# The low part of a weight unit, formed by a negated copy and an accumulating transfer

## The chip, the cores and the metric

The kernel runs on one core of a Trainium2 chip. The metric is the device time of one execution in microseconds (us), the median of several runs. The core has five engines with a queue each, which run at the same time and wait for each other by semaphores: TensorE (PE; its weight loads are shown as PEld), VectorE (DVE), ScalarE (ACT), GpSimd (POOL) and SyncE (SP). Sixteen DMA engines move data between the HBM and the SBUF. A transfer is issued from an engine's queue and tells by a semaphore that it has landed.

## The reference

One layer of a hybrid decoder, in float32, for 512 prompt tokens and 8 x 8 sample tokens, 576 in all, with a width of 1024. Cut to what matters:

```python
xn = rms_norm(h, g_mix)
z = xn @ w_in                                   # 1024 x 6144
b, c, hc, v = z[..., :o1], z[..., o1:o2], z[..., o2:o3], z[..., o3:o4]
gate_a, gate_b = sigmoid(z[..., o4:o5]), sigmoid(z[..., o5:])
ya, cb = gated_short_conv(b, c, hc, conv_buf, w_conv)
ya = ya @ w_out_conv                            # 1024 x 1024
yb, pb = multiscale_pool(v, pool_buf, pos0, w_pool, pool_scale)
h = h + (gate_a * ya + gate_b * yb) @ w_o       # 1024 x 1024
h = h + square(relu(rms_norm(h, g_mlp) @ w_up)) @ w_down   # 1024 x 4096, 4096 x 1024
gp = sigmoid(rms_norm(h, g_ple) @ w_ple_gate)   # 1024 x 1024
h = h + gp * (p @ w_ple_proj)                   # 256 x 1024
return rms_norm(h, g_final), new_conv, new_pool
```

The outputs are the tokens after the final norm and the new states of the convolution and of the pooling.

## The kernel before

The tokens stand in the free dimension, two halves of 288 columns, and the channels on the 128 partitions. A product of one tile of 128 output channels (`product`, L104) sums over eight operand tiles of 128 channels each. Every float32 operand is used as two parts, a = hi + lo, in the type float32r: `mm` (L93) multiplies hi x hi, then weight-hi x operand-lo, then weight-lo x operand-hi, for both halves. That makes 6 matmuls per operand tile and 48 per product.

The weights come as a stream of 139 units in the order of their use (L134 to L149). A unit holds what one product needs, 128 x 1024 numbers (512 KB); a unit of `w_pool` has 128 x 512 and serves two products of two operand tiles each, so 24 matmuls, and a unit of `w_pp` serves four such products. `Stream.next` (L127) is called at each product. It loads units ahead (`load_unit`, from SyncE's queue into one of four `raw` tiles) and splits the unit that will be used two products later. `split_unit` (L86) calls `split` (L66): ScalarE casts the raw unit to `hi`, and VectorE subtracts `hi` from the raw unit into `lo`. There are three `hi` and three `lo` tiles, so that unit u+3 can be written only when the matmuls of unit u are done. Five units near the end (`resident`) are split in halves into tiles of another pool by `split_unit_acts` (L89).

The stages run in this order: the first norm with three products whose weights are loaded apart as `fraw` (PSUM tiles `psf`); 21 units of the gated convolution; 8 of its gate and 8 of its output; four groups of the pooling branch with two pool units, two gate units and one `w_pool` unit each; 8 of the output projection; the MLP with four blocks of 8 up and 8 down units; the embedding with 2 units of `w_pp` and 8 of `w_pg`. After a product, ScalarE and VectorE take it out of the PSUM, work on it and split the result by `split_act` for the next stage; GpSimd sums squares for the norms (`ss`) and copies pieces of the states. A scheduler in the framework orders each engine's instructions from the program, so the order of a queue isn't always that of the code; the instructions of one engine run in that order, and one that waits holds what is behind it.

Of the kernel before, what the change touches and what calls it, by code (L numbers as in the profile page):

```python
# [8 lines left out]
F32R = mybir.dt.float32r  # L9
AF = mybir.ActivationFunctionType  # L10
ALU = mybir.AluOpType

P = 128
# [26 lines left out]
def tile_hybrid_step(ctx: ExitStack, tc: tile.TileContext, x, pt, vecs, rc, ident, sconv, spool, w_first, w_in,  # L40
                     w_pool, w_oc, w_o, w_up, w_down, w_pg, w_pp,
                     y_out, ncp, npp, ncs, nps):
    nc = tc.nc
# [5 lines left out]
    wsp = ctx.enter_context(tc.tile_pool(name="wsp", bufs=3))  # L49
# [12 lines left out]
    def as32(ap):  # L62
        return ap.bitcast(F32)

# [1 line left out]
    def split(src, shape, pool, tag, scale=None, hi_from=None):  # L66
        hi = pool.tile(shape, F32R, tag=tag, name="hi")
        lo = pool.tile(shape, F32R, tag=tag if pool is acts else tag + "l", name="lo")
        if scale is None:
            nc.scalar.copy(hi, src)  # L70
            nc.vector.tensor_tensor(out=lo, in0=src, in1=as32(hi), op=ALU.subtract)  # L71
        else:
            nc.scalar.mul(hi, src, scale)  # L73
            nc.vector.scalar_tensor_tensor(  # L74
                out=lo, in0=src, scalar=scale, in1=as32(hi), op0=ALU.mult, op1=ALU.subtract)
        return hi, lo
# [4 lines left out]
    def load_unit(ap):  # L81
        raw = wraw.tile([P, ap.shape[1]], F32, tag="raw", name="raw")
        nc.sync.dma_start(raw, ap)
        return raw

    def split_unit(raw):  # L86
        return [split(raw, [P, raw.shape[1]], wsp, "w")]

    def split_unit_acts(raw):  # L89
        n = raw.shape[1] // 2  # L90
        return [split(raw[:, i * n:(i + 1) * n], [P, n], acts, "act") for i in range(2)]

    def mm(outs, w, c, m, act, start, stop):  # L93
        """outs: pieces of PSUM, each with the part of the operand's columns that it belongs to."""
        n = w[0][0].shape[-1]
        wh, wl = (t[:, c % n:c % n + m] for t in w[c // n])
        for i, (wt, at) in enumerate(((wh, act[0]), (wh, act[1]), (wl, act[0]))):
            for o, cols in outs:
                nc.tensor.matmul(o, wt, cols(at), start=start and i == 0, stop=stop and i == 2)  # L99

    def both(ps):
        return [(ps[:, h, :HT], lambda t, h=h: t[:, h, :]) for h in range(NH)]

    def product(unit, operands, base=0, m=P, step=P):  # L104
        """One tile of outputs on partitions: sum over the operand tiles."""
        ps = psum.tile([P, NH, 512], F32, tag="ps", name="ps")
        n = len(operands)
        for k, a in enumerate(operands):
            c = base + k * step
            mm(both(ps), unit, c, m, a, k == 0, k == n - 1)  # L110
        return ps

# [1 line left out]
    class Stream:  # L114
        def __init__(self, aps, ahead=2, resident=()):
            self.resident = resident
# [3 lines left out]
        def fill(self, loads, splits):  # L120
            while len(self.raws) < min(loads, len(self.aps)):
                self.raws.append(load_unit(self.aps[len(self.raws)]))
            while len(self.parts) < min(splits, len(self.aps)):
                i = len(self.parts)
                self.parts.append((split_unit_acts if i in self.resident else split_unit)(self.raws[i]))

        def next(self):  # L127
            self.fill(self.used + 1 + self.ahead + 1, self.used + 1 + self.ahead)
# [19 lines left out]
    order += [w_pg[j] for j in range(NJ)]  # L148
    stream = Stream(order, resident=range(len(order) - NJ, len(order) - 3))  # L149

# [1 line left out]
    vec = const.tile([P, NV, NJ], F32, tag="vec", name="vec")  # L152
    nc.scalar.dma_start(vec, vecs)

# [6 lines left out]
    for j in range(NJ):  # L161
# [4 lines left out]
        if j % 2 == 0:  # L166
            raw = wraw.tile([P, 2, 3 * P], F32, tag="raw", name="fraw")
# [16 lines left out]
    xg, first = [], []  # L184
    for j in range(NJ):
        if j == 0:
            hi, lo = (acts.tile([P, NH, HT], F32R, tag="act", name=n) for n in ("hi", "lo"))
# [17 lines left out]
    sp = const.tile([P, NJ, DB, PB], F32, tag="sp", name="sp")  # L205
    nc.sync.dma_start(sp, spool)

# [1 line left out]
    class Rms:  # L209
        def __init__(self, n=NH, width=HT, chunk=HT // 3):  # L210
            self.n, self.width, self.chunk, self.parts = n, width, chunk, []
# [14 lines left out]
                self.parts[0] = s  # L226

        def tokens(self):
            """Sums with tokens on partitions, and 1 / rms there."""
            n, m = len(self.at), self.chunk  # L230
            self.ps = ps = psum.tile([P, NH, 512], F32, tag="ps", name="psn")
            sums = ps[:m, 0, self.width:self.width + n]
            for i, (h, c) in enumerate(self.at):
                for k, a in enumerate(self.parts):
                    nc.tensor.matmul(  # L235
                        sums[:, i:i + 1], a[:, h, c:c + m], ones32[:, 0:1],
                        start=k == 0, stop=k == len(self.parts) - 1)
            rt, ms, y, t = (tmp.tile([m, n], F32, tag=g, name=g, bufs=2) for g in ("rt", "ms", "ry", "rz"))
            nc.scalar.activation(rt, sums, AF.Sqrt, bias=epst[:m], scale=1.0 / D)
            nc.vector.tensor_scalar(out=ms, in0=sums, scalar1=1.0 / D, scalar2=EPS, op0=ALU.mult, op1=ALU.add)  # L240
            nc.vector.reciprocal(y, rt)
            nc.vector.tensor_tensor(out=t, in0=y, in1=y, op=ALU.mult)
            nc.vector.scalar_tensor_tensor(out=t, in0=t, scalar=-0.5, in1=ms, op0=ALU.mult, op1=ALU.mult)
            nc.vector.scalar_tensor_tensor(out=y, in0=t, scalar=1.5, in1=y, op0=ALU.add, op1=ALU.mult)
            self.y = y

        def spread(self):
            """The same on all partitions, in PSUM."""
            m = self.chunk
            for i, (h, c) in enumerate(self.at):  # L250
                nc.tensor.matmul(  # L251
                    self.ps[:, h, c:c + m], self.y[:, i:i + 1].broadcast_to([m, P]), idt[:m, :m],
                    start=True, stop=True)
            return self.ps[:, :self.n, :self.width]
# [7 lines left out]
            nc.scalar.activation(out2, r, AF.Square)  # L262
            return out, out2

# [1 line left out]
    stat = Rms()  # L266
    for j in range(NJ):
        stat.add(xs[j])
# [1 line left out]
    for k in range(NJ):  # L270
        for u in range(3):
            mm(both(ps0[u]), [first[k]], u * P, P, xg[k], k == 0, k == NJ - 1)
        if k == 5:
            stat.tokens()
        if k == 6:
            r1, r1s = stat.copies(stat.spread(), "r", "rs")
# [1 line left out]
    ncp_t = const.tile([P, NJ, CW - 1], F32, tag="ncp", name="ncp_t")  # L278
    npp_t = const.tile([P, NJ, PB], F32, tag="npp", name="npp_t")

# [1 line left out]
    ya_in = []  # L282
    for j in range(NJ):
        ps_c = ps0[0] if j == 0 else product(stream.next(), xg)
        c = tmp.tile([P, NH, HT], F32, tag="t", name="c")
        nc.vector.tensor_tensor(out=c, in0=halves(ps_c), in1=r1s, op=ALU.mult)
        ps_h = ps0[1] if j == 0 else product(stream.next(), xg)
        u = tmp.tile([P, CEXT], F32, tag="ext", bufs=4, name="u")
        us = u[:, CE:].rearrange("p (b t) -> p b t", b=DB)
# [13 lines left out]
        for k in range(1, CW):  # L303
            nc.vector.scalar_tensor_tensor(
                out=cv[:, :n], in0=u[:, k:k + n], scalar=v(W_CONV + k, j), in1=cv[:, :n],
                op0=ALU.mult, op1=ALU.add)
        ps_b = ps0[2] if j == 0 else product(stream.next(), xg)
        bt = tmp.tile([P, NH, HT], F32, tag="t", name="bt")
        nc.vector.tensor_tensor(out=bt, in0=halves(ps_b), in1=r1, op=ALU.mult)
# [8 lines left out]
            op=ALU.mult)  # L318
        ya_in.append(split_act(ya))

# [1 line left out]
    mix = []  # L322
    for j in range(NJ):
        ps = product(stream.next(), xg)
        z = tmp.tile([P, NH, HT], F32, tag="t", name="z")
# [5 lines left out]
        ps = product(stream.next(), ya_in)  # L331
        nc.vector.tensor_tensor(out=mix[j], in0=halves(ps), in1=mix[j], op=ALU.mult)

# [1 line left out]
    merged = []  # L335
    for g, w in enumerate(WINDOWS):
        pooled = []
        for i in range(2):
# [14 lines left out]
            s, d = e, 1  # L353
            while d < w:
                q = tmp.tile([P, PEXT], F32, tag="ext", bufs=4, name="q")
                lo = 2 * d - 1
                nc.vector.tensor_tensor(
                    out=q[:, lo:], in0=s[:, lo:], in1=s[:, lo - d:PEXT - d], op=ALU.add)
                s, d = q, 2 * d
# [19 lines left out]
        for i in range(2):  # L379
            ps = product(stream.next(), xg)  # L380
            z = tmp.tile([P, NH, HT], F32, tag="t", name="zb")
# [14 lines left out]
    for o, t in ((ncp, ncp_t), (ncs, sc), (npp, npp_t), (nps, sp)):  # L396
        nc.sync.dma_start(o, t)

# [1 line left out]
    stat = Rms()  # L400
    hg = []
    for j in range(NJ):
# [2 lines left out]
        hg.append(split_act(xs[j], v(G_MLP, j)))  # L405
        stat.add(xs[j])

# [1 line left out]
    accs = [None] * NJ  # L409
    stat3 = Rms()  # L410
    hg2 = []
    for b in range(NFB):
        sq = []
        for j in range(NJ):
# [5 lines left out]
            a = tmp.tile([P, NH, HT], F32, tag="t", name="a")  # L420
# [20 lines left out]
                hg2.append(split_act(xs[j], v(G_PLE, j)))  # L441
                stat3.add(xs[j])

# [1 line left out]
    proj = []  # L445
    for i in range(2):
        w = stream.next()
# [23 lines left out]
    for h, (a, b) in enumerate(((0, cut), (cut, NT))):  # L471
        for j in range(NJ):
# [10 lines left out]
            z = tmp.tile([P, 1, b - a], F32, tag="t", name="z1")  # L483
# [98 lines left out]
```

## Time and profile before

| | before |
|---|---|
| median of 3 runs (range) | 927.73 us (927.15 to 928.21) |
| span of the profiled execution, first to last instruction | 926.5 us |
| its mean granted TensorE clock | 0.994 |
| DMA: bytes read from HBM, written | 77.01 MB, 2.99 MB |
| DMA: mean rate over the span | 87 GB/s |

The profile is of one execution on the chip; its own time beyond the span is not recorded, and the median of the runs lies 1.2 us above the span. In the profile's lines a group reads "line engine operation out<-in", with the shape and type, how many times it ran, its busy time and the mean of one, and the engine's idle time just ahead of it with what ended that. In a timeline a row begins with its start and its duration in us. In the slices a digit is the busy share of a fortieth of the span in tenths.

### The profile page before, as it was taken

How to read it: one execution, taken by the hardware profiler on the slowest of the kernel's cores; microseconds unless marked ns; L12 is line 12 of the kernel's file. 1: busy time of each engine (PE TensorE's matmuls, PEld its weight loads, DVE VectorE, ACT ScalarE, POOL GpSimd, SP SyncE). 2: the span in 40 equal slices, each digit the busy share in tenths (PEclk: the TensorE clock that was granted, in tenths of full speed). 3: DMA queues.
4: the chain of work that ended last, by engine and by line, in shares of the span. 5: the costliest groups of instructions: out<-in, count | busy, mean ns of one | idle time of the engine just before them, and what ended most of it. 6: DMA issues, size and time to landing. Idle time of an engine off the chain costs nothing.

```text
span 926.5 us, 15543 instructions
## 1 busy us (share of the span) xinstructions
PE 913.4 (99%) x6842; PEld 911.5 (98%) x6842; DVE 431.6 (47%) x570; ACT 289.8 (31%) x384; POOL 98.3 (11%) x118
## 2 busy tenths in 40 slices
PE   8999999999999999999999999999999999999995
PEld 7999999999999999999999999999999999999995
DVE  7645445333246687743342133332443334567555
ACT  6422212322113222333433233211331133335532
POOL 5110001000011221023000000000000000021253
PEclk9999999999999999999999999999999999999997
DMA  6422222322322222322222222222222222222102
GB/s 227 155 92 76 84 92 69 94 88 73 92 61 88 68 92 96 112 79 91 69 90 71 91 79 82 91 70 91 87 73 92 74 86 92 94 92 84 54 22 82
DMA packets 26290, 80.98 MB, mean 87 GB/s; under 512 B 3312, under 2 KB 7024, under 8 KB 26224
## 3 DMA queue, kind: packets, MB, share of 16 engines
q1 hardware_dynamic: 26080, 79.98, 26.4%
q8 instruction: 53, 0.87, 0.4%
q14 instruction: 13, 0.11, 0.0%
q10 hardware_dynamic: 144, 0.03, 0.0%
HBM read 77.01 MB, written 2.99 MB: 86 GB/s over the span
## 4 chain that ended last, share of the span: by engine, by line
PE 97%; DVE 1%; issue 1%; DMA 1%; SPq 0%; DVEq 0%; ACT 0%; ACTq 0%
PE ps L99 89%; PE psg L99 6%; PE psf L99 1%; PE psn L251 1%; DVE lo L71 1%; DMA xall<-x 1%; PE psn L235 1%; DVE xall L464 0%; SPq L169 0%; DVE lo L74 0%; SPq L163 0%; DVEq L564 0%; DVE gp L491 0%; DVE xall L493 0%; DVE sq L218 0%
## 5 line engine op out<-in xcount | busy, mean ns | idle before, releaser
L99 PE MATMUL ps<-lo,hi 128*128 128x288 f32 x2064 | 442.2, 296 | 0.0
L99 PE MATMUL ps<-hi 128*128 128x288 f32 x2064 | 442.1, 296 | 0.0
L99 PE MATMUL ps<-hi,lo 128*128 128x288 f32 x2064 | 441.8, 296 | 0.0
L99 PEld LDWEIGHTS ps<-hi,lo 128*128 128x128 f32 x2064 | 332.7, 189 | 0.0
L99 PEld LDWEIGHTS ps<-lo,hi 128*128 128x128 f32 x2064 | 332.7, 189 | 0.0
L99 PEld LDWEIGHTS ps<-hi 128*128 128x128 f32 x2064 | 332.6, 189 | 0.0
L70 ACT CAST hi<-raw 128x1024 fp32r<-128x1024 f32 (+1 forms) x144 | 144.8, 1008 | 468.3 <-PE ps L99 400.9
L71 DVE TENSOR_TENSOR lo<-raw,hi 128x1024 fp32r<-128x1024 f32 (+1 forms) x144 | 169.3, 1179 | 157.0 <-ACT hi L70 150.4
L437 DVE TENSOR_TENSOR acc<-ps,acc 128x576 f32<-128x576 f32 x24 | 18.2, 758 | 74.3 <-PE ps L99 74.3
L225 POOL TENSOR_TENSOR ss<-sq 128x576 f32<-128x576 f32 (+2 forms) x5 | 7.2, 1434 | 416.4 <-ACT sq L220 416.4
L225 POOL TENSOR_TENSOR ss<-ss,sq 128x576 f32<-128x576 f32 (+2 forms) x29 | 38.5, 1327 | 70.3 <-ACT sq L220 56.8
L99 PE MATMUL psg<-hi 128*128 128x320 f32 (+1 forms) x128 | 38.1, 298 | 0.0
L99 PE MATMUL psg<-lo,hi 128*128 128x320 f32 (+1 forms) x128 | 37.9, 296 | 0.0
L99 PE MATMUL psg<-hi,lo 128*128 128x320 f32 (+1 forms) x128 | 37.9, 296 | 0.0
L71 DVE TENSOR_TENSOR lo<-a,hi 128x576 fp32r<-128x576 f32 x32 | 24.3, 759 | 23.6 <-ACT hi L70 23.6
L70 ACT CAST hi<-a 128x576 fp32r<-128x576 f32 x32 | 21.6, 675 | 43.6 <-DVE a L423 43.6
L220 ACT ACTIVATE sq<-xall 128x576 f32<-128x576 f32 (+2 forms) x39 | 22.7, 585 | 19.5 <-DVE xall L493 19.5
L74 DVE SCALAR_TENSOR_TENSOR lo<-xall,vec,hi 128x576 fp32r<-128x576 f32 x23 | 21.7, 946 | 7.9 <-ACT hi L73 7.9
L99 PEld LDWEIGHTS psg<-hi 128*128 128x128 f32 x128 | 24.3, 190 | 0.0
L99 PEld LDWEIGHTS psg<-lo,hi 128*128 128x128 f32 x128 | 24.3, 190 | 0.0
L99 PEld LDWEIGHTS psg<-hi,lo 128*128 128x128 f32 x128 | 24.3, 190 | 0.0
L423 DVE TENSOR_TENSOR a<-a 128x576 f32<-128x576 f32 x32 | 24.1, 752 | 0.0
(98 smaller groups left out, 444.3 us busy)
## 6 DMA issues: line engine op xcount, KB each, us to landing
raw<-w_in SPq DMA_DIRECT2D x45, 512.0 KB, 3.4
raw<-w_up SPq DMA_DIRECT2D x32, 512.0 KB, 3.4
raw<-w_down SPq DMA_DIRECT2D x32, 512.0 KB, 3.5
raw<-w_oc SPq DMA_DIRECT2D x8, 512.0 KB, 3.4
raw<-w_o SPq DMA_DIRECT2D x8, 512.0 KB, 3.5
raw<-w_pg SPq DMA_DIRECT2D x8, 512.0 KB, 3.5
xall<-x SPq DMA_DIRECT2D x7, 288.0 KB, 5.2
fraw<-w_first SPq DMA_DIRECT2D x8, 192.0 KB, 5.1
```

What stands on the lines that cost most here:

```text
L70: nc.scalar.copy(hi, src)
L71: nc.vector.tensor_tensor(out=lo, in0=src, in1=as32(hi), op=ALU.subtract)
L74: nc.vector.scalar_tensor_tensor(out=lo, in0=src, scalar=scale, in1=as32(hi), op0=ALU.mult, op1=ALU.subtract)
L99: nc.tensor.matmul(o, wt, cols(at), start=start and i == 0, stop=stop and i == 2)
L220: nc.scalar.activation(sq, t, AF.Square)
L225: nc.gpsimd.tensor_tensor(out=s, in0=self.parts[0], in1=sq, op=ALU.add)
L235: nc.tensor.matmul(sums[:, i:i + 1], a[:, h, c:c + m], ones32[:, 0:1], start=k == 0, stop=k == len(self.parts) - 1)
L251: nc.tensor.matmul(self.ps[:, h, c:c + m], self.y[:, i:i + 1].broadcast_to([m, P]), idt[:m, :m], start=True, stop=True)
L423: nc.vector.tensor_tensor(out=a2, in0=a, in1=a, op=ALU.mult)
L437: nc.vector.tensor_tensor(out=accs[j], in0=halves(ps), in1=accs[j], op=ALU.add)
```

## The change

`split_unit` no longer calls `split`. ScalarE writes `hi` as before, and then writes the raw unit times -1 into `lo`, rounded to float32r as `hi` is, so that `lo` holds minus `hi`. A transfer issued from GpSimd's queue then reads the unit from the HBM a second time and adds it to what stands in `lo`. The subtraction on VectorE is gone for the 134 units that go this way; the five resident units, the first weights `fraw` and all activations are split as before. The comments that the diff takes out of other places have no effect and are left out here.

```diff
-    def split_unit(raw):
-        return [split(raw, [P, raw.shape[1]], wsp, "w")]
+    def split_unit(raw, ap):
+
+        shape = [P, raw.shape[1]]
+        hi = wsp.tile(shape, F32R, tag="w", name="hi")
+        lo = wsp.tile(shape, F32R, tag="wl", name="lo")
+        nc.scalar.copy(hi, raw)
+        nc.scalar.mul(lo, raw, -1.0)
+        nc.gpsimd.dma_start(lo, ap, accum_op=ALU.add)
+        return [(hi, lo)]
...
             while len(self.parts) < min(splits, len(self.aps)):
                 i = len(self.parts)
-                self.parts.append((split_unit_acts if i in self.resident else split_unit)(self.raws[i]))
+                if i in self.resident:
+                    self.parts.append(split_unit_acts(self.raws[i]))
+                else:
+                    self.parts.append(split_unit(self.raws[i], self.aps[i]))
```

The changed lines move the numbers of all lines behind them: in the changed kernel L91 is the cast to `hi` of a unit, L92 the negated copy into `lo`, L93 the transfer, and what stood at L225 or L384 is L235 or L394.

ScalarE at the start of the stream, before. `raw` is a weight unit, `rt` belongs to the first norm, and `r` and `rs` are its copies from the PSUM:

```order
L70 CAST hi<-raw 128x1024
L239 ACT_TABLE_LOAD
L239 ACTIVATE rt<-psn,epst 96x6
L70 CAST hi<-raw 128x1024
L258 COPY r<-psn 128x576
L262 ACTIVATE rs<-psn 128x576
L70 CAST hi<-raw 128x1024
```

The same place in the changed kernel:

```order
L91 CAST hi<-raw 128x1024
L249 ACT_TABLE_LOAD
L249 ACTIVATE rt<-psn,epst 96x6
L92 ACTIVATE lo<-raw 128x1024
L91 CAST hi<-raw 128x1024
L92 ACTIVATE lo<-raw 128x1024
L268 COPY r<-psn 128x576
L272 ACTIVATE rs<-psn 128x576
L91 CAST hi<-raw 128x1024
L92 ACTIVATE lo<-raw 128x1024
```

The first negated copy stands behind `rt`, and the second one ahead of `r`.

GpSimd at the same place, before: the sums of squares of the first norm, and pieces of the convolution's state (`u`, `sc`, `ncp_t`):

```order
L225 TENSOR_TENSOR ss<-ss,sq 128x576 x6
L291 COPY u<-sc 128x8x2
L298 COPY ncp_t<-u 128x2
L299 COPY sc<-u 128x16
L290 MEMSET u 128x2
```

In the changed kernel:

```order
L235 TENSOR_TENSOR ss<-ss,sq 128x576 x6
L301 COPY u<-sc 128x8x2
L93 DMA lo<-w_in 128x1024 x2
L308 COPY ncp_t<-u 128x2
L93 DMA lo<-w_in 128x1024
L309 COPY sc<-u 128x16
L300 MEMSET u 128x2
```

Two transfers are issued ahead of the copy that waits for the convolution's first tile, and the third one behind it.

ScalarE in the last group of the pooling branch, before. `pl` is an operand of the group's last product, `gb` a gate, `t` a merged result:

```order
L70 CAST hi<-raw 128x512
L70 CAST hi<-pl 128x576
L70 CAST hi<-raw 128x1024
L384 ACTIVATE gb<-zb 128x576
L70 CAST hi<-pl 128x576
L70 CAST hi<-raw 128x1024
L384 ACTIVATE gb<-zb 128x576
L70 CAST hi<-raw 128x1024
L70 CAST hi<-t 128x576 x2
```

In the changed kernel, from the cast of the same `w_pool` unit on:

```order
L91 CAST hi<-raw 128x512
L92 ACTIVATE lo<-raw 128x512
L91 CAST hi<-raw 128x1024
L70 CAST hi<-pl 128x576
L394 ACTIVATE gb<-zb 128x576
L92 ACTIVATE lo<-raw 128x1024
L91 CAST hi<-raw 128x1024
L92 ACTIVATE lo<-raw 128x1024
L394 ACTIVATE gb<-zb 128x576
L91 CAST hi<-raw 128x1024
L70 CAST hi<-t 128x576
L92 ACTIVATE lo<-raw 128x1024
```

The negated copy of the unit that is cast right after the `w_pool` unit stands behind the operand `pl` and the gate `gb`; the next one stands right behind its cast.

## The prediction

> **What bounds the kernel now.** I read the page's busy shares and slices first, then the chain that ended last, in order of time.
>
> ```profile
> span 926.5 us, 15543 instructions
> PE 913.4 (99%) x6842; PEld 911.5 (98%) x6842; DVE 431.6 (47%) x570; ACT 289.8 (31%) x384; POOL 98.3 (11%) x118
> PE   8999999999999999999999999999999999999995
> PEclk9999999999999999999999999999999999999997
> ```
>
> ```profile
> 29.06 2.02 PE psf L99 x15
> 31.08 409.60 PE ps L99 x3072
> ...
> 861.37 33.22 PE psg L99 x234
> ...
> 899.27 14.81 PE psg L99 x123
> 914.10 0.43 DVE z L484
> ```
>
> TensorE is busy in every slice but the first and the last, at full clock, and from 29 to 914 us the chain is matmuls alone: 3072 of them stand in one piece. VectorE, which the change relieves, has no step in the chain between 29 and 914 us. So nothing can be won in the middle, and the question is only whether TensorE comes to wait for a low part. The pace is 409.60 / 3072 = 0.1333 us a matmul, 6.40 us for a unit of 48, and 3.20 us for a unit of w_pool with 24. The first matmuls that read a low part are the fifth and sixth of a unit, 0.53 us after its start.
>
> **What is removed and added.** These are the two groups that split, from the page; a group with "+1 forms" mixes shapes.
>
> ```profile
> L70 ACT CAST hi<-raw 128x1024 fp32r<-128x1024 f32 (+1 forms) x144 | 144.8, 1008 | 468.3 <-PE ps L99 400.9
> L71 DVE TENSOR_TENSOR lo<-raw,hi 128x1024 fp32r<-128x1024 f32 (+1 forms) x144 | 169.3, 1179 | 157.0 <-ACT hi L70 150.4
> ```
>
> Of the 144, 10 are halves of the five resident units and stay; 134 go. VectorE loses about 134 x 1.2 = 160 us, all of it beside matmuls: worth nothing. ScalarE gets 134 negated copies. The trace has none; I take 1.05 us, the cast of the same shape below, since a relu and a cast of 576 columns there take 0.65 and 0.68. ScalarE goes from 290 to about 430 us of 926, still far from a bound. GpSimd's queue and the DMA engines get 134 accumulating transfers, which read the weights from HBM a second time.
>
> **The unknown: T, from issue to landing of one accumulating transfer.** The trace has no such transfer and none issued by GpSimd; every queue in it that carries data is a hardware one. The nearest rows:
>
> ```profile
> raw<-w_in SPq DMA_DIRECT2D x45, 512.0 KB, 3.4
> xall<-x SPq DMA_DIRECT2D x7, 288.0 KB, 5.2
> raw<-w_pool SPq DMA_DIRECT2D x4, 256.0 KB, 2.7
> q1 hardware_dynamic: 26080, 79.98, 26.4%
> ```
>
> 512 KB plain lands in 3.4 us, 256 KB in 2.7: so 2.0 fixed and 1.4 per 512 KB. The lowest value is 3.4, if reading the old contents and adding were free. With two reads of 512 KB side by side it is 2.0 + 2.8 = 4.8; with the two passes one behind the other 2 x 3.4 = 6.8. The slowest pace of a large load in the trace is 288 KB in 5.2 us; 1 MB at that pace takes 18 us, my upper end. Between these I take the middle of the two forms of a second pass, T = 5.8, nearest to the row of the same unit, and keep 3.4 and 18.
>
> [...]
>
> **Where T is hidden: the regular stages.** ScalarE in the MLP:
>
> ```profile
> 641.19 1.05 ACT L70 CAST hi<-raw 128x1024 fp32r<-128x1024 f32 x1 [5.35 <-PE ps L99]
> 647.59 1.05 ACT L70 CAST hi<-raw 128x1024 fp32r<-128x1024 f32 x1 [5.35 <-PE ps L99]
> 648.55 0.65 ACT L421 ACTIVATE a<-ps 128x576 f32<-128x576 f32 x1
> 650.60 0.68 ACT L70 CAST hi<-a 128x576 fp32r<-128x576 f32 x1 [1.41 <-DVE a L423]
> ```
>
> The high part of unit u+3 starts when unit u ends (three buffers), here at 647.59. Units u+1 and u+2 then run 2 x 6.40, and the low part is read at 647.59 + 12.80 + 0.53 = 660.9. In the changed order the relu stands between the cast and the negated copy: 647.59 + 1.05 + 0.65 + 1.05 = 650.3, when the transfer is issued. It is hidden as long as T is under 10.6. Behind it on GpSimd in this stage stand only the next units' transfers; in the stages with `ss` sums or state copies these wait at most for the issue, and their readers are a unit away.
>
> **Where it is tightest: the pool stage,** since a unit of w_pool is half as long. First ScalarE, then one row of TensorE:
>
> ```profile
> 373.30 1.05 ACT L70 CAST hi<-raw 128x1024 fp32r<-128x1024 f32 x1 [4.48 <-PE ps L99]
> 374.84 0.69 ACT L384 ACTIVATE gb<-zb 128x576 f32<-128x576 f32 x1 [0.49 <-DVE zb L382]
> 375.43 0.66 ACT L70 CAST hi<-pl 128x576 fp32r<-128x576 f32 x1
> 379.70 1.05 ACT L70 CAST hi<-raw 128x1024 fp32r<-128x1024 f32 x1 [3.60 <-issue]
> ...
> 389.30 1.05 ACT L70 CAST hi<-raw 128x1024 fp32r<-128x1024 f32 x1 [1.86 <-PE ps L99]
> ```
>
> ```profile
> 383.45 0.43 PE L99 MATMUL ps<-hi,lo 128*128 128x288 f32 x2
> ```
>
> The unit whose high part starts at 373.30 has its low part read at 383.45. In the new order two more ScalarE instructions come ahead of its negated copy: 373.30 + 1.05 + 0.66 + 0.69 + 1.05 = 376.8, so T up to 6.6 is hidden. The next one starts at 379.70 and its product at 389.30: 389.30 + 0.53 - (379.70 + 2.10) = 8.0. The three earlier groups have no pool operand between and stand at 8.0 too. With 5.8 this stage costs nothing; 0.8 us is what the first place has to spare.
>
> **Where it is not hidden: the first stream unit.** ScalarE, then VectorE, GpSimd and TensorE:
>
> ```profile
> 23.70 1.05 ACT L70 CAST hi<-raw 128x1024 fp32r<-128x1024 f32 x1 [3.07 <-DVE lo L71]
> 24.77 1.28 ACT L239 ACT_TABLE_LOAD   x1
> 26.06 0.26 ACT L239 ACTIVATE rt<-psn,epst 96x6 f32<-96x6 f32 x1
> 27.12 1.05 ACT L70 CAST hi<-raw 128x1024 fp32r<-128x1024 f32 x1 [0.80 <-PE psf L99]
> 29.09 0.64 ACT L258 COPY r<-psn 128x576 f32<-128x576 f32 x1 [0.93 <-PE psn L251]
> 29.63 0.66 ACT L262 ACTIVATE rs<-psn 128x576 f32<-128x576 f32 x1
> ```
>
> ```profile
> 24.78 1.23 DVE L71 TENSOR_TENSOR lo<-raw,hi 128x1024 fp32r<-128x1024 f32 x1 [0.62 <-ACT hi L70]
> 30.38 0.76 DVE L286 TENSOR_TENSOR c<-psf,rs 128x576 f32<-128x576 f32 x1 [0.95 <-ACT rs L262]
> ```
>
> ```profile
> 21.28 0.54 POOL L291 COPY u<-sc 128x16 f32<-128x16 f32 x1
> ```
>
> ```profile
> 30.92 0.43 PE L99 MATMUL ps<-hi 128*128 128x288 f32 x2
> 31.45 0.43 PE L99 MATMUL ps<-hi,lo 128*128 128x288 f32 x2
> ```
>
> Before, the low part of the first unit is done at 24.78 + 1.23 = 26.0, and TensorE reads it at 31.45. After, the negated copy stands behind `rt` and ends at 26.32 + 1.05 = 27.4; GpSimd is free since 21.8 and issues. What stays hidden is 31.45 - 27.4 = 4.0 us. With T = 5.8 the part lands at 33.2: **TensorE waits 1.8 us**. The second negated copy delays `r` and `rs`: the second cast moves from 27.12 to 27.4, then 28.5, copy to 29.5, `r` and `rs` together 1.2 to 30.7. TensorE starts the unit at 30.92, so this costs nothing, and `c` about 0.4 us later is not waited for before the next product. The second unit is read 6.40 later, at 37.9: its transfer, issued at 29.5, has 8.4. Once the stream has slipped by 1.8 us it is not caught up, since TensorE has no idle time to give back.
>
> The sum against the profiled execution: 926.5 + 1.8 = 928.3. The median of the runs shown, 927.73, lies 1.2 above its span, so **929.5**, 0.2% more. About 0.2% (1.9 us) is what a measurement of this kernel can tell from no change, and the forecast lies right on that bound.
>
> **The rivals.**
> - *No wait, hence not slower.* T is 4.0 or less, the adding being free as in the lowest end: the first unit lands before 31.45, time 927.7. For it speaks that a plain load has 3.4; against it the second read. It decides at T = 4.0, at 31.45 us.
> - *Later than the pool stage allows.* T between 6.6 and 10.6. At T = 9 the first unit costs 5.0, the last group 2.4, and the other three groups 1.0 each (the second unit of a group is carried by the slip of the first): 10.4 us, 938. At 10.6 it is 6.6 + 4.0 + 7.8 = 18.4, 946.
> - *The transfers become the bound.* T over 10.6, or more engine time than there is: loads take 26.4% of 926.5, some 1.75 us for each of 139 units, so an accumulating one has 6.40 - 1.75 = 4.6, 2.6 times a load. Past that, each us costs 134 / 3 = 45 us: 1010 at T = 12, and near 1280 at my upper end of 18. Against it: two reads make 2, not 2.6.
> - *A shared port.* Beside GpSimd's sum a VectorE subtraction took three times as long:
>
> ```profile
> 4.34 0.56 DVE L71 TENSOR_TENSOR lo<-fraw,hi 128x384 fp32r<-128x384 f32 x1
> 10.33 1.78 DVE L71 TENSOR_TENSOR lo<-fraw,hi 128x384 fp32r<-128x384 f32 x1
> ```
>
> ```profile
> 9.96 1.73 POOL L225 TENSOR_TENSOR ss<-ss,sq 128x576 f32<-128x576 f32 x1 [0.18 <-ACT sq L220]
> ```
>
> If issuing a transfer is held up likewise for one VectorE instruction, 1.2 us, T is 7.0 where VectorE is busy. At the first unit only short steps on 96 x 6 numbers are left on VectorE, so the price is 0.4 us at the last pool group: 929.9. [...]
> - *Faster.* Only if a lighter VectorE ended a wait on the chain; the chain has none between 29 and 914 us.
>
> **How the numbers follow.** Forecast (T 4.0 to 6.6, 927.7 to 930.3) 0.45; no wait 0.10; shared port 0.05; pool stage late 0.18; transfers the bound 0.19; faster 0.03. A second read is close to certain, hence the weight on the forecast, but a first transfer of a kind that the trace does not have can be far dearer than its bytes, hence the last cases. Of the forecast half lies on each side of T = 5.8: same is 0.10 + 0.22 = 0.32, slower 0.23 + 0.05 + 0.18 + 0.19 = 0.65, faster 0.03. The range of the likeliest case is 927.7 to 930.3; over all it reaches from 927.0 up to the end of the pool-stage case, 948, which leaves out 0.03 below and most of the 0.19 above.
>
> **What would show it.** Right: issue-to-landing of `lo<-w_in` near 5.8 us, one wait of TensorE near 31.5 us of T - 4.0, released by that transfer, and no other; ScalarE near 430 us; DMA share about 26% plus a half to the double of it. Wrong: waits of TensorE every third unit (T over 10.6), or in the pool stage (over 6.6), a GpSimd that is long busy with each issue, or no wait at all.

## The result, and the profile after

| | before | changed |
|---|---|---|
| median of four runs each (range), us | 927.73 (927.15 to 928.21) | 937.53 (933.01 to 939.09) |
| span of the profiled execution, us | 926.5 | 937.3 |
| mean granted TensorE clock | 0.994 | 0.991 |

The changed kernel is slower: the ratio is 1.0096, with a 95% interval of 1.0069 to 1.0123, so 9 us at the middle; the medians lie 9.8 us apart. The profiled execution of the changed kernel is the slowest of its four. The forecast was 929.5, in a range of 927.0 to 948.0.

The page of the changed kernel, its head and its slices:

```profile
span 937.3 us, 15857 instructions
PE 917.3 (98%) x6842; PEld 914.4 (98%) x6842; DVE 278.8 (30%) x436; ACT 408.6 (44%) x518; POOL 195.4 (21%) x252
PE   8799999999999999999999999999999999999995
PEclk9899999999999999999999999999999999999997
```

VectorE has lost 153 us of work and ScalarE has gained 119, and neither matters. What matters is one slice of TensorE that fell from 9 to 7, and one of its clock that fell from 9 to 8. The waits of TensorE for transfers follow, with total, times and the longest; then the transfers, with their number, size and median time from issue to landing:

```profile
PE ps L106 <- DMA lo<-w_in: 5.4, 2, 5.3
PE ps L106 <- DMA lo<-w_o: 1.6, 1, 1.6
```

```profile
q0 software_dynamic: 19296, 69.21, 42.2%
q1 hardware_dynamic: 26080, 79.98, 28.5%
raw<-w_in SPq DMA_DIRECT2D x45, 512.0 KB, 4.1
lo<-w_in POOLq DMA_DIRECT2D x45, 512.0 KB, 7.6
lo<-w_pg POOLq DMA_DIRECT2D x3, 512.0 KB, 5.6
lo<-w_pool POOLq DMA_DIRECT2D x4, 256.0 KB, 5.4
```

T, the time from issue to landing of an accumulating transfer, is 7.6 us here, and 5.6 for the last three, of `w_pg`. The three waits listed add up to 7.0 us, and none is listed for any other of the 134 transfers. The chain of work names transfers that ended late:

```profile
27.52 9.39 DMA lo<-w_in
...
361.73 8.11 DMA lo<-w_in
...
385.96 8.11 DMA lo<-w_o
```

How much of the loss lies where is read from the starts of the products' readers (minimum, median and maximum of their duration in ns, then the first and the last start in us). First two rows of before, then two of the changed kernel:

```profile
L286 DVE TENSOR_TENSOR c<-ps,rs x7: 751/757/757, 37.7 to 152.7; 128x576 f32<-128x576 f32 x7
L404 DVE TENSOR_TENSOR xall<-ps,xall x8: 758/758/758, 389.5 to 434.3; 128x576 f32<-128x576 f32 x8
```

```profile
L296 DVE TENSOR_TENSOR c<-ps,rs x7: 758/758/758, 45.7 to 160.9; 128x576 f32<-128x576 f32 x7
L414 DVE TENSOR_TENSOR xall<-ps,xall x8: 758/758/758, 400.3 to 445.1; 128x576 f32<-128x576 f32 x8
```

The first stream unit is finished 45.7 - 37.7 = 8.0 us later than before, the last of this stage 160.9 - 152.7 = 8.2 later, and the first unit of the output projection 400.3 - 389.5 = 10.8 later, which is the whole difference of the spans (937.3 - 926.5). So 8.0 to 8.2 us are lost at the first unit and 2.6 by the end of the pool stage, and next to nothing elsewhere. In the pool stage TensorE's matmuls halt at 340, 369 and 392 us, for 0.16, 0.13 and 1.57 us by the timeline, and each halt costs 0.2 to 0.3 us more than that: the first two matmuls behind it take 0.52 to 0.54 instead of 0.42 us. At the first unit the matmuls that read the low part start at 36.95 instead of 31.45 us, so the wait explains 5.5 of the 8.0. TensorE's timeline and its clock in two stretches show the rest:

```profile
31.27 0.42 PE L106 MATMUL ps<-lo,hi 128*128 128x288 f32 x2
36.95 0.85 PE L106 MATMUL ps<-hi,lo 128*128 128x288 f32 x2 [5.25 <-DMA lo<-w_in]
37.59 0.68 PE L106 MATMUL ps<-hi 128*128 128x288 f32 x2
...
43.06 0.42 PE L106 MATMUL ps<-hi 128*128 128x288 f32 x2
```

```profile
37.00:40.00 3.00, 3.00 (x13) 3.00 (x14) 0.76 (x1) 0.00 (x0) 0.00 (x0) 0.50 1.05 277
43.00:46.00 3.00, 3.00 (x25) 3.00 (x24) 0.35 (x1) 0.58 (x1) 0.00 (x0) 1.00 0.00 0
```

In the second fence the columns are the stretch, its length, the busy time of PE, PEld, DVE, ACT and POOL with the number of instructions, the granted clock, the DMA share and the GB/s. After the wait two matmuls take 0.68 instead of 0.42 us; from 37 to 40 us only 13 matmuls run where 25 run later, at a clock of 0.50. By 43 us the clock is whole again. 8.0 - 5.5 = 2.5 us are lost in this. That the wait is the cause of the slow clock is tested below by the busy gap.

### The profile page after: what moved, and what is told of

Same layout as the page of the kernel before. It is cut to its first block, busy times and chain, and to the rows that moved or that the text cites. A ratio compares the mean times of both kernels' runs of the same rounds, so it can differ in the third digit from the quotient of the medians.

```text
span 937.3 us, 15857 instructions
## 1 busy us (share of the span) xinstructions
PE 917.3 (98%) x6842; PEld 914.4 (98%) x6842; DVE 278.8 (30%) x436; ACT 408.6 (44%) x518; POOL 195.4 (21%) x252
## 3 DMA queue, kind: packets, MB, share of 16 engines
q0 software_dynamic: 19296, 69.21, 42.2%
q1 hardware_dynamic: 26080, 79.98, 28.5%
## 4 chain that ended last, share of the span: by engine, by line
PE 90%; issue 3%; DMA 3%; DVE 1%; POOL 1%; ACT 0%; SPq 0%; DVEq 0%; POOLq 0%; ACTq 0%
PE ps L106 84%; PE psg L106 5%; DMA lo<-w_in 2%; DMA lo<-w_o 1%; DVE lo L71 1%; PE psn L261 1%; PE psf L106 0%; PE psn L245 0%; DMA xall<-x 0%; POOL lo L93 0%; POOL sp L362 0%; DVE xall L474 0%; POOL e L354 0%; ACT hi L73 0%; ACT sq L230 0%
## 5 line engine op out<-in xcount | busy, mean ns | idle before, releaser
L91 ACT CAST hi<-raw 128x1024 fp32r<-128x1024 f32 (+1 forms) x134 | 139.1, 1038 | 450.0 <-issue 419.1
L92 ACT ACTIVATE lo<-raw 128x1024 fp32r<-128x1024 f32 (+1 forms) x134 | 139.6, 1041 | 0.0
L93 POOL DMA_DIRECT2D lo<-w_in x45 | 39.0, 867 | 182.2 <-ACT lo L92 175.9
L93 POOL DMA_DIRECT2D lo<-w_up x32 | 27.7, 865 | 174.2 <-ACT lo L92 161.2
L93 POOL DMA_DIRECT2D lo<-w_down x32 | 27.7, 865 | 168.8 <-ACT lo L92 168.8
L235 POOL TENSOR_TENSOR ss<-ss,sq 128x576 f32<-128x576 f32 (+2 forms) x29 | 36.1, 1244 | 24.6 <-ACT sq L230 21.4
```

What stands on the lines that cost most here:

```text
L91: nc.scalar.copy(hi, raw)
L92: nc.scalar.mul(lo, raw, -1.0)
L93: nc.gpsimd.dma_start(lo, ap, accum_op=ALU.add)
L235: nc.gpsimd.tensor_tensor(out=s, in0=self.parts[0], in1=sq, op=ALU.add)
```

## The experiments

Each run changes one thing in the changed kernel. Theory A was: the loss is a few late landings at fixed places, and the first of them also halves TensorE's clock. Theory B: the added traffic or ScalarE slows the whole kernel a little. For the length of T, theory R held the second read of the memory responsible and theory I GpSimd's issue and its queue; and for what the forecast's T had missed, theory C the load that runs beside each accumulating transfer, against rival N, that 7.6 us are the transfer's own.

**The first unit by VectorE.** In `fill`:

```diff
                 if i in self.resident:
                     self.parts.append(split_unit_acts(self.raws[i]))
+                elif i in (0,):
+                    raw = self.raws[i]
+                    self.parts.append([split(raw, [P, raw.shape[1]], wsp, "w")])
                 else:
```

> Only the first stream unit is split by VectorE again; the other 133 keep the accumulating transfer. Theory A (the loss is a few late landings at fixed places, and the first one also halves TensorE's clock for some microseconds): the wait of 5.3 us at 31.5 us and the slow matmuls behind it go, 8.0 of the 10.8 us; what stays are the two waits of the last pool group, 2.5 us: span 929.0 to 929.6, time about 930.5, same. Theory B (transfers or ScalarE slow TensorE everywhere by a little): only the 5.3 us go, span 932.

Measured: 928.98 us beside 927.81 of before on the same chip, ratio 1.0013 (1.0005 to 1.0022), span 926.9. TensorE's waits in it:

```profile
PE ps L106 <- DMA lo<-w_o: 1.0, 1, 1.0
PE ps L106 <- DMA lo<-w_in: 0.2, 1, 0.2
```

Taking one transfer of 134 away gives back 8 of the 9 us. The time is 1.2 us above before, about what the two remaining waits add up to. It was a little less than A had expected, since those waits were 1.2 us here and not 2.5; B, with 932, falls.

**The first unit and the eight units behind a w_pool unit by VectorE.** The same edit with `i in (0, 42, 43, 47, 48, 52, 53, 57, 58)`.

> The first unit and the eight units that follow a w_pool unit (first and second unit of groups 2 to 4 and of the output projection) are split by VectorE; the other 125 keep the accumulating transfer. Theory A: no wait of TensorE on a transfer is left, span 926.5 and time 927.7 as before, within 0.1%. Theory B: still 2 us or more above before, since 125 transfers remain.

Measured: 927.42 beside 927.81, ratio 0.9997 (0.9988 to 1.0006). No wait of TensorE on a transfer is left; its longest ones are those of the norms:

```profile
PE psn L248 <- POOL ss L238: 1.7, 2, 1.0
PE psn L248 <- DVE sq L231: 1.4, 1, 1.4
```

125 accumulating transfers that nobody waits for cost nothing that these runs can tell: at most 0.06%, or 0.6 us. Theory A holds. And 125 fewer subtractions on VectorE gain nothing: no version tried has a median clear below that of before.

**A busy gap.** 39 matmuls with zero weights stand between the fourth and the fifth matmul of the first stream unit (`fillers` is 39 for that unit alone):

```diff
         for i, (wt, at) in enumerate(((wh, act[0]), (wh, act[1]), (wl, act[0]))):
+            if i == 2 and fillers:
+                o, cols = outs[0]
+                for _ in range(fillers.pop()):
+                    nc.tensor.matmul(o, zero, cols(act[0]), start=False, stop=False)
```

> The changed kernel with 39 more matmuls of 288 columns with zero weights, between the fourth and the fifth matmul of the first stream unit; they add zero. They take 39 x 0.133 = 5.2 us, about the wait. Clock theory (TensorE's clock is halved because it stood still for 5 us): the low part still lands near 36.9 us, but the matmuls behind it run at 0.133 us instead of 0.24 and the granted clock stays at 1.00 until the end; span 2.5 us less than the changed kernel's, about 934.8. Rival (the slow stretch comes from the DMA engines being full at 30 to 40 us, which slows TensorE's reads): the matmuls behind the landing stay at 0.24 us and the span at 937.

Measured: 934.08 beside 927.81, ratio 1.0067 (1.0053 to 1.0080); the changed kernel had 1.0096. TensorE's timeline at the place:

```profile
31.59 5.31 PE L110 MATMUL ps<-hi,zero 128*128 128x288 f32 x39
36.73 0.51 PE L112 MATMUL ps<-hi,lo 128*128 128x288 f32 x2
37.09 0.42 PE L112 MATMUL ps<-hi 128*128 128x288 f32 x2
```

The real matmuls go on at 36.73 us, where the changed kernel has 36.95, but at 0.51 and then 0.42 us for two, and the mean clock is 0.996. The DMA engines have the same work in both: the first three accumulating transfers are issued at 27.57, 29.45 and 33.34 us, where the changed kernel has 27.52, 29.39 and 33.28, and the slice of the page from 23 to 47 us has a DMA share of 7 tenths in both. So the slow stretch came from standing still, and not from the DMA engines. The last two matmuls of the unit start at 42.41 us, where the changed kernel has 45.18: 2.8 us come back at this place, 0.2 of them by the earlier start. The times alone would not show it, since the two intervals, 1.0053 to 1.0080 and 1.0069 to 1.0123, overlap.

**No accumulation.** The transfer overwrites, so `lo` is the weight itself and the subtraction is left out:

```diff
-        nc.gpsimd.dma_start(lo, ap, accum_op=ALU.add)
+        nc.gpsimd.dma_start(lo, ap)
```

> The same transfers from GpSimd without the add: they overwrite the low part with the weight, so the subtraction is left out; all waits stay. Theory R (the second read sets the landing): issue to landing falls from 7.6 us to that of the plain load, 4.1, and GpSimd's issue of 0.9, about 5.0; the first unit waits 1 to 2 us and the pool stage nothing: span 927.5 to 929. Theory I (writing the descriptors on GpSimd and its queue set it): landing stays above 6.5 us and the span above 933.

Measured: 931.22 us in one run, span 929.4. These are its lines of the transfers and of TensorE:

```profile
q0 software_dynamic: 19296, 69.21, 20.9%
lo<-w_in POOLq DMA_DIRECT2D x45, 512.0 KB, 4.5
```

```profile
33.35 0.85 PE L106 MATMUL ps<-hi,lo 128*128 128x288 f32 x2 [2.96 <-DMA lo<-w_in]
34.00 0.68 PE L106 MATMUL ps<-hi 128*128 128x288 f32 x2
...
36.78 0.43 PE L106 MATMUL ps<-hi 128*128 128x288 f32 x2
```

Landing falls from 7.6 to 4.5, and the engines' time for the same bytes from 42.2% to 20.9%, by half: an accumulating transfer costs the DMA engines two plain ones here. So it is the accumulation and not the issue by GpSimd that makes the landing long, as theory R had it; whether the second read takes the time or the adding itself, this run doesn't separate. R's time was half a microsecond to two too low, since the first unit still waited 3.0 and the clock was halved here too, for about 3.4 us. Its transfer was issued at 26.20 and read at 33.35, about 7.1 us later and not 4.5, although it did not add: the start is crowded without the add too, with a DMA share of 0.99 from 28 to 30 us and of 0.70 to 1.34 in the three stretches of 1 us behind. GpSimd's part is small: its issue takes 0.53 us in the middle instead of 0.86.

**The negated copy reads the high part,** so that the raw buffer is free one ScalarE instruction sooner:

```diff
-        nc.scalar.mul(lo, raw, -1.0)
+        nc.scalar.mul(lo, as32(hi), -1.0)
```

> The negated copy reads the high part and not the raw unit, so the raw buffer is free, and the load that waits for it is issued, about 1.05 us sooner; the result is the same. Theory C (the accumulating transfer is stretched by the load of a later unit that the same ScalarE instruction sets free, so that both run at once): the load is half done when the transfer starts, landing falls from 7.6 to 6.3 to 6.9 us, the waits of the last pool group shrink from 2.5 to under 1.2 us, time 934 to 937. Rival N (the landing is the transfer's own, whatever runs beside it): 7.6 us and 937.5 stay.

What made this worth trying are two rows of the changed kernel, of SyncE's and of GpSimd's queue: the load of a later unit (the first of the four in the row) and the accumulating transfer go out 0.3 us apart, set free by the same negated copy.

```profile
105.06 19.53 SPq L83 DMA_DIRECT2D raw<-w_in  x4
```

```profile
105.32 0.86 POOL L93 DMA_DIRECT2D lo<-w_in  x1 [5.53 <-ACT lo L92]
```

Measured: 935.15 beside 927.65, ratio 1.0071 (1.0057 to 1.0085).

```profile
lo<-w_in POOLq DMA_DIRECT2D x45, 512.0 KB, 6.5
lo<-w_up POOLq DMA_DIRECT2D x32, 512.0 KB, 5.5
```

For the 512 KB units of the long stages landing falls to 5.5 to 6.5, and the waits of the pool stage are gone. The first unit still waits 3.5 us and still has a slow stretch behind it, at a clock of 0.50 from 34 to 37 us. C holds, N falls. The profile is of the fastest of the four runs (932.25); the others lie 2.5 to 3.4 us above it, and their waits are not known.

**The loads behind the accumulating transfers,** in the same queue: in `fill` the loads are made after the splits and issued by GpSimd; the first three loads stay in SyncE's queue. The main part of the edit:

```diff
+            while splits and len(self.raws) < min(loads, len(self.aps)):
+                self.raws.append(load_unit(self.aps[len(self.raws)], nc.gpsimd))
```

> The loads of later units are issued from GpSimd's queue too, each behind the accumulating transfer of the unit that frees its buffer. Theory C: the transfer has the DMA engines first, and lands like the last three of the changed kernel, which have no load beside them, in 5.4 to 6.0 us; no wait in the pool stage; the first unit lands in under 7.5 us and waits 2.5 to 3.5 us, with one slow stretch or none; time 930 to 933. Rival N: landing 7.6, time 937.

Measured: 929.68 beside 927.65, ratio 1.0013 (0.9991 to 1.0036); ten runs, nine of them from 929.5 to 932.3 and one at 919.7, which I can't explain and which pulls the ratio down. The transfers, and TensorE at the first unit:

```profile
lo<-w_in POOLq DMA_DIRECT2D x45, 512.0 KB, 5.3
raw<-w_in POOLq DMA_DIRECT2D x42, 512.0 KB, 6.3
```

```profile
32.80 0.52 PE L106 MATMUL ps<-hi,lo 128*128 128x288 f32 x2 [1.01 <-DMA lo<-w_in]
33.17 0.42 PE L106 MATMUL ps<-hi 128*128 128x288 f32 x2
```

With no load ahead of it T is 5.3 to 5.5 in the middle for the 512 KB units of every stage. The load now takes 6.3 instead of 4.1, and TensorE waits for none. The one wait left is 1.0 us, without a slow stretch behind it: less than C had expected.

**The same, with the first unit by VectorE.**

> As the kernel before it in this list, with the first unit split by VectorE. Theory C: no wait on a transfer is left, time within 0.1% of before, 927.2 to 928.6. Rival N: the waits of the last pool group stay, 929 to 930.5.

Measured: 928.16 beside 927.65, ratio 1.0004 (0.9995 to 1.0013). No wait on a transfer is left, as C had it.

## Why the prediction was right in its direction, and off in its size

- **The bound.** Right. TensorE sets the time; the relief of VectorE is worth nothing (927.42 beside 927.81, and 928.16 beside 927.65, with few of the stream's splits left on it); time is lost only where TensorE waits for a low part.
- **The places.** Right as a list. The first unit, read at 31.45 us with 4.0 us to spare, and the pool stage, with 6.6 us to spare at its tightest unit, were named, and no other place showed a wait of note. But the forecast had a wait only at the first, and named waits in the pool stage as a sign of being wrong: what came is its rival "later than the pool stage allows", to which it gave 0.18, and not its likeliest case. At the second place, ScalarE's and GpSimd's rows of the changed kernel are the ones that the order let expect:

```profile
382.51 1.05 ACT L91 CAST hi<-raw 128x1024 fp32r<-128x1024 f32 x1 [5.53 <-issue]
383.46 0.67 ACT L70 CAST hi<-pl 128x576 fp32r<-128x576 f32 x1
384.03 0.68 ACT L394 ACTIVATE gb<-zb 128x576 f32<-128x576 f32 x1
384.62 1.05 ACT L92 ACTIVATE lo<-raw 128x1024 fp32r<-128x1024 f32 x1
```

```profile
385.96 0.86 POOL L93 DMA_DIRECT2D lo<-w_o  x1 [6.69 <-ACT lo L92]
```

  Cast, pool operand, gate, negated copy, issue: 3.45 us from the cast to the issue, where the sum had 3.45. T of 8.1 less the 6.6 to spare is 1.5; the wait was 1.6.
- **T, the term that failed.** The forecast took 5.8, "the middle of the two forms of a second pass", from rows of loads that had nothing of its kind beside them, in a kernel whose loads take 26.4% of the DMA engines' time. Alone, an accumulating transfer lands in 5.3 (with the loads behind it), nearer to the reads side by side (4.8) than to the two passes one behind the other (6.8). But in the changed kernel it is nearly never alone: the negated copy that starts it also frees the raw buffer, and the load that waits for that buffer starts 0.3 us ahead. That makes 7.6, and 9.4 for the first unit, with its several loads in flight. So the wait at the first unit was 5.3 and not 1.8. That the start is crowded stood in the profile of before, where the DMA share (the last figure but one) was 0.82 around the moment of the first issue, and 0.26 later on; the forecast took one T for both places:

```profile
24.00:30.00 6.00, 6.00 (x53) 6.00 (x53) 3.35 (x8) 4.25 (x6) 0.00 (x0) 1.00 0.82 287
...
200.00:340.00 140.00, 140.00 (x1053) 140.00 (x1052) 67.56 (x96) 33.14 (x39) 12.92 (x22) 1.00 0.26 82
```

- **The total, in part luck.** The rival of the pool stage had 938 us at T = 9, near the measured 937.5, but with a different split: its 10.4 us were 5.0 at the first unit and 5.4 in the pool stage, and what ran had 5.5, 2.5 of slow clock and 2.6. At the 8.1 us that the pool stage showed, its own sum gives 4.1 + 1.5 + 3 x 0.1 = 5.9 us, so 933.6; the rest is the longer T of the first unit and the clock. The range up to 948 held the result because it took this rival in; the likeliest case's range, 927.7 to 930.3, did not.
- **The clock, a term that was missing.** The sum took a wait at its length. A wait of 3.0 or 5.3 us was followed by matmuls at half the clock; the busy gap gave 45.18 - 42.41 = 2.8 us back at this place, 0.2 of them by its earlier start.
- **The add.** Without it the transfer issued by GpSimd landed in 4.5 us beside the loads and in 3.8 for the last three, with no load behind them; with it in 7.6 and 5.6. The DMA engines' time for the same bytes was 20.9% without it and 42.2% with it. The second read behind the forecast's T was its author's estimate: no run shows it apart from the adding.
- **The rivals.** "No wait" and "transfers become the bound" fell: the DMA share was 42.2 + 28.5 = 71%, and the regular stages with 10.6 us to spare had no wait. The rival named a shared port fell as well: GpSimd's issue takes 853, 862 and 1037 ns at least, in the middle and at most for the 45 units of `w_in`, and the means of the other groups are 863 to 877 ns. The longest is that of the first transfer, at 27.5 us, while VectorE was idle; no issue beside VectorE's work was held up by the 1.2 us that this rival needs:

```profile
L93 POOL DMA_DIRECT2D lo<-w_in x45: 853/862/1037, 27.5 to 371.3; - x45
```

## What to carry to other kernels

Here work that was taken off an engine with time to spare gained nothing, and what replaced it counted by its latency at the places with the least slack. So find that place first (the start of a stream, a short unit in it), and leave the quick path there. When a new transfer is estimated from the rows of an old one, look at what the same instruction sets free: here it freed a buffer too, so a load nearly always ran beside the transfer and stretched it from 5.3 to 7.6 us. Ask also how busy the DMA engines are at the place in question. TensorE's waits on a transfer of 3.0 us and more were followed by slow matmuls here, so that the one of 5.3 us cost 8.0.

## What the runs showed of the hardware that was not expected

- The halved clock. Waits on a transfer of 5.3 us (the changed kernel), 3.5 (the negated high part) and 3.0 (no accumulation) were followed by matmuls at a clock of 0.50; those of 1.6 us and less were not. Added up from the granted clock of 1 us stretches, the clock stood at half for 6.8 us in the first, from 35.9 to 42.7, and for 3.4 in the last, from 33.2 to 36.6. In the last it fell 0.1 us before the matmuls came back, in the first 1.1 us before; no run shows what sets the two lengths. Nor does the length of one wait decide it alone: at the end of both kernels, where TensorE has few matmuls, its clock falls to 0.50 during a wait of 1.4 us for VectorE, which follows one of 0.7 for GpSimd (from 916.2 us on in before, from 926.7 in the changed kernel). The four runs of the changed kernel spread over 6 us (933.01 to 939.09), where those of before spread over 1. Their mean clocks are 0.995, 0.993, 0.991 and 0.991 from the fastest to the slowest. A stretch of 3.4 us at half the clock takes 0.5 x 3.4 / 937 = 0.002 from the mean, one of 6.8 us twice that, so the spread may come from a slow stretch whose length differs from run to run. This is a hint and not shown: the clock of before, without a wait on a transfer, varies from 0.994 to 0.997 itself.
- An accumulating transfer took the DMA engines twice a plain one's time (42.2% against 20.9% for the same bytes). The profile has 69.21 MB for the queue in both runs, which is what the 134 units hold, so the bytes don't show what the add costs.
- Which of two transfers is stretched depends on how they are issued: with the loads in GpSimd's queue behind the accumulating transfers, the transfers took 5.3 and the loads 6.3 us; in two queues with the load ahead, 7.6 and 4.1. Whether the order alone does it or the shared queue too is open, since no run had the load behind in a queue of its own.
